# A streaming relu-mean: 127 rows a partition, and the first 128 rows one to a partition

## Chip, cores, metric

One core of one Trainium2 chip. The metric is device time of a run in microseconds (us). All runs were at a granted clock of 1.0. A ratio is the mean time of one kernel's runs over that of the other's of the same rounds, so it is not quite the ratio of the medians that are quoted beside it; brackets give its 95% interval.

## The reference

```python
x = np.random.randn(32, 512, 1024).astype(np.float32)
def reference(x):
    return np.mean(np.maximum(x, 0), axis=-1).astype(np.float32)   # 16384 rows of 1024
```

64 MiB come in, 64 KiB go out, and each element is used once. Loads and stores are moved by 16 DMA engines in packets; a packet here is one contiguous piece, such as the 16 rows of one partition.

## The kernel before

Partition p owns the 128 rows 128p to 128p+127. They are loaded in seven tiles of 16 rows a partition (8.39 MB, one packet of 64 KB a partition) through three buffers, then in pieces of 8, 4, 2, 1 rows and one last row in three column pieces. Odd rows go to VectorE, even rows to ScalarE; each row is one instruction that takes the maximum with zero and sums. GpSimd scales the sums (the last row is scaled in its own instruction). One store of 512 B a partition ends the kernel.

```python
    J = R // P                                   # 128
    xr = xf.rearrange("(p j) d -> p j d", p=P, j=J)
    outr = out.flatten().rearrange("(p j) -> p j", p=P, j=J)
    NB, BUFS = 16, 3
    full = J // NB - 1                           # 7
    row_pieces, col_pieces = [8, 4, 2, 1], [512, 256, 256]
    # ... (cut: buffers and semaphores)
    for t in range(full):
        buf_free(t)                              # waits for ScalarE and VectorE on tile t-3
        load(t, bufs[t % BUFS][:, :, :], xr[:, t * NB:(t + 1) * NB, :])
    # ... (cut: the loads of the pieces)
    nc.gpsimd.memset(scale[:, :], inv).then_inc(pool, 1)

    def rows(i, xt, lo, n, j0):
        nc.scalar.wait_ge(loaded[i], 16)
        nc.vector.wait_ge(loaded[i], 16)
        for k in range(lo, lo + n):
            j = j0 + k
            done = (dve_row if j % 2 else act_row)(nc, xt[:, k, :], sums[:, j:j + 1])
            # ... (cut: the last row of each engine raises its semaphore)
    # ... (cut: finish(), which scales sums into res on GpSimd; the last two rows)
    nc.sync.dma_start(out=outr, in_=res[:, :]).then_inc(stored, 16)
```

The first load is moved ahead of the entry barrier, so it is issued at time 0 of the span.

## Time and profile before

| | before |
|---|---|
| median of 3 runs | 162.33 us (162.28 to 162.63) |
| profiled span | 161.1 us |
| load queue, share of 16 engines' span | 97.3% |
| VectorE / ScalarE busy | 46% / 43% |

The page shows a stream: the load queue is hardly ever idle, and the two compute engines wait for it. The prediction shows the page's lines, the table of stretches and the drain. It lacks the moments at which tiles arrive, by which the kernels are compared later. Here they are for the kernel before, as VectorE's first instruction on each of the first four tiles in the timeline (start, duration, instruction, and in brackets the idle time that the tile's arrival ended):

```profile
22.45 1.22 DVE L20 TENSOR_SCALAR_CACHE_REDUCE rows<-rows 128x1024 f32<-128x1024 f32 x1 [22.45 <-DMA rows<-in_x_dram]
...
41.71 1.22 DVE L20 TENSOR_SCALAR_CACHE_REDUCE rows<-rows 128x1024 f32<-128x1024 f32 x1 [10.05 <-DMA rows<-in_x_dram]
...
61.15 1.22 DVE L20 TENSOR_SCALAR_CACHE_REDUCE rows<-rows 128x1024 f32<-128x1024 f32 x1 [10.24 <-DMA rows<-in_x_dram]
...
81.01 1.22 DVE L20 TENSOR_SCALAR_CACHE_REDUCE rows<-rows 128x1024 f32<-128x1024 f32 x1 [10.65 <-DMA rows<-in_x_dram]
```

From 41.71 to 61.15 is 19.44 us and from 61.15 to 81.01 is 19.86; the later tiles take 19.34 to 19.36. Ten idle microseconds a tile are VectorE's slack.

### The profile page before, as it was taken

What the parts mean: (1) busy time and instruction counts of PE and PEld (TensorE: products, weight loads), DVE (VectorE), ACT (ScalarE), POOL (GpSimd) and SP (SyncE); (2) the same over time, 40 slices, a digit from 0 to 9 for tenths busy, and PEclk for the clock granted to TensorE, in tenths of its full rate; (3) what the DMA queues carried; (4) which work ended last, traced back from release to release, by engine and by line L of the source; (5) the groups of instructions that cost most, each with busy time, mean ns of one, the idle gap of its engine ahead of it and who ended that gap; (6) DMA issues with size and microseconds to landing.
All of it is one profiled execution on the core that took longest, in us unless ns stands there. A gap on an engine that the chain in (4) does not pass through costs nothing. (4 is left out here: it accounts for less than half of the span.)

```text
span 161.1 us, 336 instructions
## 1 busy us (share of the span) xinstructions
DVE 74.3 (46%) x132; ACT 69.2 (43%) x131; POOL 1.3 (1%) x8
## 2 busy tenths in 40 slices
DVE  0000049800696008940089400992029900498994
ACT  3000049600694008920089200990029800496974
POOL 1000000000000000000000000000000000000001
DMA  7997997997997998999999999999999999899991
GB/s 260 521 472 309 521 472 309 521 456 325 521 439 342 521 423 358 525 391 391 521 391 391 505 407 391 505 407 391 505 407 391 505 407 391 382 464 391 409 401 52
DMA packets 2162, 67.19 MB, mean 417 GB/s; under 512 B 240, under 2 KB 624, under 8 KB 880
## 3 DMA queue, kind: packets, MB, share of 16 engines
q1 hardware_dynamic: 2160, 67.18, 97.3%
q14 instruction: 2, 0.02, 0.0%
HBM read 67.11 MB, written 0.07 MB: 417 GB/s over the span
## 5 line engine op out<-in xcount | busy, mean ns | idle before, releaser
L20 DVE TENSOR_SCALAR_CACHE_REDUCE rows<-rows 128x1024 f32<-128x1024 f32 x64 | 73.3, 1208 | 84.8 <-DMA rows<-in_x_dram 84.6
L15 ACT ACTIVATE rows<-rows 128x1024 f32<-128x1024 f32 x64 | 66.2, 1036 | 88.2 <-DMA rows<-in_x_dram 88.0
L15 ACT ACTIVATION_READ_ACCUMULATOR rows<-rows 128x1 f32 x64 | 11.9, 187 | 0.0
L20 DVE DVE_READ_ACCUMULATOR rows<-rows 128x1 f32 x64 | 5.3, 83 | 0.0
L15 ACT ACT_TABLE_LOAD x1 | 1.3, 1283 | 1.4 <-PEq L55 1.4
L132 POOL TENSOR_SCALAR res<-sums 128x112 f32<-128x112 f32 (+1 forms) x2 | 0.5, 250 | 155.5 <-DVE rows L20 155.5
L15 ACT ACTIVATE last<-last 128x512 f32<-128x512 f32 x1 | 0.6, 629 | 0.0
L20 DVE TENSOR_SCALAR_CACHE_REDUCE last<-last 128x256 f32<-128x256 f32 x1 | 0.4, 420 | 0.2 <-DMA last<-in_x_dram 0.2
L165 DVE SCALAR_TENSOR_TENSOR last<-last,scale 128x258 f32<-128x258 f32 x1 | 0.4, 428 | 0.1
L117 POOL MEMSET scale<- 128x258 f32 x1 | 0.3, 313 | 1.0 <-POOLq L55 1.0
L155 POOL TENSOR_SCALAR res<-part 128x1 f32<-128x1 f32 x1 | 0.3, 264 | 0.6 <-DVE rows L20 0.6
L15 ACT ACTIVATION_READ_ACCUMULATOR last<-last 128x1 f32 x1 | 0.2, 186 | 0.0
L195 POOL MEMSET const-bfloat16-1.0<- 128x1 bf16 x1 | 0.1, 102 | 0.0
L195 POOL MEMSET const-uint8-127<- 128x1 uint8 x1 | 0.1, 102 | 0.0
L195 POOL MEMSET const-float32-0.0<- 128x1 f32 x1 | 0.1, 99 | 0.2 <-issue 0.2
L195 POOL MEMSET const-float32-1.0<- 128x1 f32 x1 | 0.1, 99 | 0.0
L20 DVE DVE_READ_ACCUMULATOR last<-last 128x1 f32 x1 | 0.1, 83 | 0.0
L165 DVE DVE_READ_ACCUMULATOR last<-last,scale 128x1 f32 x1 | 0.1, 82 | 0.0
## 6 DMA issues: line engine op xcount, KB each, us to landing
rows<-in_x_dram SPq DMA_DIRECT2D x1, 4096.0 KB, 39.1
rows<-in_x_dram SPq DMA_DIRECT2D x1, 2048.0 KB, 43.6
rows<-in_x_dram SPq DMA_DIRECT2D x1, 1024.0 KB, 45.6
rows<-in_x_dram SPq DMA_DIRECT2D x1, 512.0 KB, 46.5
last<-in_x_dram SPq DMA_DIRECT2D x1, 256.0 KB, 46.6
last<-in_x_dram SPq DMA_DIRECT2D x2, 128.0 KB, 46.4
rows<-in_x_dram SPq DMA_DIRECT2D x7, 49.2
out_dram<-res SPq DMA_DIRECT2D x1, 64.0 KB, 1.5
```

Source lines behind the costliest of these rows:

```text
L15: return nc.scalar.activation(out=src, in_=src, func=ACT.Relu, accum_out=acc)
L20: return nc.vector.tensor_scalar(out=src, in0=src, scalar1=0.0, scalar2=init, op0=ALU.max, op1=ALU.add, accum_out=acc,)
L117: nc.gpsimd.memset(scale[:, :], inv).then_inc(pool, 1)
L132: nc.gpsimd.tensor_scalar(out=res[:, lo:hi], in0=sums[:, lo:hi], scalar1=inv, scalar2=0.0, op0=ALU.mult, op1=ALU.add,)
L155: nc.gpsimd.tensor_scalar(out=res[:, J - 2:J - 1], in0=part[:, 0:1], scalar1=part[:, 1:2], scalar2=inv, op0=ALU.add, op1=ALU.mult,).then_i ...
L165: nc.vector.scalar_tensor_tensor(out=last[:, 768:], in0=last[:, 768:], scalar=0.0, in1=scale[:, :], op0=ALU.max, op1=ALU.mult, accum_out=r ...
L195: nc = _bacc.Bacc("TRN2", target_bir_lowering=False, num_devices=1)
```

## The change

The intent is a row pitch between partitions that is no power of two: 127 rows of 4 KiB (508 KiB) in place of 128 (512 KiB). That leaves 128 rows over. They are loaded one to a partition behind tile 0, averaged by one ScalarE instruction that scales as well, turned from a column into rows by a VectorE transpose, and stored in mid-stream as four runs of 32 results.

```diff
-    xr = xf.rearrange("(p j) d -> p j d", p=P, j=J)
-    outr = out.flatten().rearrange("(p j) -> p j", p=P, j=J)
+    xfirst, xmain = xf[:P, :], xf[P:, :]
+    outfirst, outmain = out.flatten()[:P], out.flatten()[P:]
+    J = J - 1
+    xr = xmain.rearrange("(p j) d -> p j d", p=P, j=J)
+    outr = outmain.rearrange("(p j) -> p j", p=P, j=J)
-    row_pieces = [8, 4, 2, 1]
+    row_pieces = [7, 4, 2, 1]
@@ loads
         load(t, bufs[t % BUFS][:, :, :], xr[:, t * NB:(t + 1) * NB, :])
+        if t == 0:
+            load(-1, row0[:, :], xfirst)
+        if t == BUFS:
+            nc.sync.wait_ge(first, 2)
+            nc.sync.dma_start(
+                out=outfirst.rearrange("(q i) -> q i", i=32), in_=turned0[0:P:32, :],
+            ).then_inc(stored, 16)
@@ compute
+    nc.gpsimd.memset(mean0[:, :], 0.0)
     nc.gpsimd.memset(scale[:, :], inv).then_inc(pool, 1)
+    nc.scalar.wait_ge(pool, 1)
     nc.vector.wait_ge(pool, 1)
     for t in range(full):
         rows(t, bufs[t % BUFS], 0, NB, t * NB)
+        if t == 0:
+            nc.scalar.wait_ge(loaded[-1], 16)
+            nc.scalar.activation(
+                out=row0[:, :], in_=row0[:, :], func=ACT.Relu, scale=inv, accum_out=mean0[:, 0:1],
+            ).then_inc(first, 1)
+            nc.vector.wait_ge(first, 1)
+            nc.vector.transpose(turned0[:, :], mean0[:, :]).then_inc(first, 1)
```

Cut: the three small buffers, one more semaphore and its place in the list that is cleared, the count of full tiles (7 as before), the last row's index, the final wait for 32 in place of 16, an assert.

More of the change, by code (lines that the diff above doesn't have):

```diff
@@ L63 @@
     inv = 1.0 / D
-    xr = xf.rearrange("(p j) d -> p j d", p=P, j=J)
-    outr = out.flatten().rearrange("(p j) -> p j", p=P, j=J)
+    xfirst, xmain = xf[:P, :], xf[P:, :]
[3 more added lines that the diff above has]
+    outr = outmain.rearrange("(p j) -> p j", p=P, j=J)
     NB = 16
     BUFS = 3
-    full = J // NB - 1
-    row_pieces = [8, 4, 2, 1]
-    assert sum(row_pieces) == NB - 1
+    full = J // NB
+    row_pieces = [7, 4, 2, 1]
+    assert full * NB + sum(row_pieces) + 1 == J
     col_pieces = [512, 256, 256]
@@ L84 @@
     scale = sbuf("scale", P, D // 4 + 2)
-    loaded = [nc.alloc_semaphore(f"loaded{i}") for i in range(full + len(row_pieces) + len(col_pieces))]
+    row0, mean0, turned0 = sbuf("row0", P, D), sbuf("mean0", P, 32), sbuf("turned0", P, 32)
+    loaded = [nc.alloc_semaphore(f"loaded{i}") for i in range(full + len(row_pieces) + len(col_pieces) + 1)]
     act, dve, pool = (nc.alloc_semaphore(n) for n in ("act", "dve", "pool"))
+    first = nc.alloc_semaphore("first")
     stored = nc.alloc_semaphore("stored")
@@ L144 @@
     finish(i, j0, j0 + lo)
-    prev = xt[:, NB - 2, :]
+    prev = xt[:, lo, :]
     nc.scalar.wait_ge(loaded[i], 16)
@@ L173 @@
     nc.sync.dma_start(out=outr, in_=res[:, :]).then_inc(stored, 16)
-    used = [s.num for s in (*loaded, act, dve, pool)]
+    used = [s.num for s in (*loaded, act, dve, pool, first)]
     assert used == list(range(used[0], used[0] + len(used)))
     nc.sync.sem_clear(range(used[0], used[-1] + 1))
-    nc.sync.wait_ge(stored, 16).then_inc(stored, -16)
+    nc.sync.wait_ge(stored, 32).then_inc(stored, -32)
     issue_ahead_of_entry_barrier(nc)
```

## The prediction

> **What bounds the kernel now.** I read the page first: busy shares, DMA rows, queue, chain, costly groups, DMA issues.
>
> ```profile
> span 161.1 us, 336 instructions
> DVE 74.3 (46%) x132; ACT 69.2 (43%) x131; POOL 1.3 (1%) x8
> ...
> q1 hardware_dynamic: 2160, 67.18, 97.3%
> ...
> HBM read 67.11 MB, written 0.07 MB: 417 GB/s over the span
> ...
> DVE 0%; issue 0%
> ...
> L20 DVE TENSOR_SCALAR_CACHE_REDUCE rows<-rows 128x1024 f32<-128x1024 f32 x64 | 73.3, 1208 | 84.8 <-DMA rows<-in_x_dram 84.6
> L15 ACT ACTIVATE rows<-rows 128x1024 f32<-128x1024 f32 x64 | 66.2, 1036 | 88.2 <-DMA rows<-in_x_dram 88.0
> ...
> rows<-in_x_dram SPq DMA_DIRECT2D x7, 49.2
> out_dram<-res SPq DMA_DIRECT2D x1, 64.0 KB, 1.5
> ```
>
> Both compute engines are under half busy and nearly all their idle time ends on a load; the load queue is busy for 97.3% of the span. The chain of waits follows the last vector instruction only and says 0%, because it does not follow the loads; it is no help here. So the question is whether the stream itself can go faster. I cut the span at the moments the tiles arrive (first instruction on each tile in the timeline: 22.3, 41.7, 61.1, 81.0, 100.4, 119.7, 139.1 us).
>
> ```profile
> core 0: us, DVE busy (x) ACT busy (x) POOL busy (x), PEclk, DMA share, GB/s
> 22.30:41.70 19.40, 9.21 (x16) 8.42 (x16) 0.00 (x0) 1.00 1.00 432
> 41.70:61.10 19.40, 9.20 (x16) 8.43 (x16) 0.00 (x0) 1.00 1.00 432
> 61.10:81.00 19.90, 9.20 (x16) 8.43 (x16) 0.00 (x0) 1.00 0.98 422
> 81.00:100.40 19.40, 9.23 (x17) 8.46 (x17) 0.00 (x0) 1.00 1.00 432
> ```
>
> A tile of 8.39 MB takes 19.35 to 19.4 us with the DMA engines fully busy; compute on it takes 9.2. One tile takes 19.9. The packet records say why: each of the 16 engines runs 64 KB packets back to back, median 2.418 us, shortest 2.415, so eight packets (8 partitions) make 19.34 us. At 65.06 to 65.46 us two 8 KB instruction fetches were taken in between; one engine lost about 1.0 us there (a gap of 0.4 and a packet of 2.99), and that very engine ends last, at 158.30 us, about 0.3 behind the next. The other loss is at the start: the first packet of each engine, beginning at 1.0 to 2.0 us, takes 2.9 to 3.5 us instead of 2.4. The end is a short drain (timeline):
>
> ```profile
> 158.46 0.42 DVE L20 TENSOR_SCALAR_CACHE_REDUCE last<-last 128x256 f32<-128x256 f32 x1 [0.25 <-DMA last<-in_x_dram]
> ...
> 158.99 0.43 DVE L165 SCALAR_TENSOR_TENSOR last<-last,scale 128x258 f32<-128x258 f32 x1
> ...
> 159.50 0.35 SPq L173 DMA_DIRECT2D out_dram<-res  x1
> ```
>
> Last bytes 158.30, usable 158.99, reduced 159.42, store issued 159.50 and landed 1.5 us later, span end 161.07. The time is about 1.0 us of start, about 157.3 of stream, about 2.8 of drain. Only the stream's bytes and rate, the last piece and the final store can move it.
>
> **What the Trainium skill says.** (1) "DMA: Bandwidth & Descriptors", section "Where 436 GB/s comes from": sixteen ports of 32 B at 850 MHz give 435.2 GB/s, and the ports bind. The trace agrees: 65,536 B in 2.418 us is 27.1 GB/s, times 16 is 433.7, or 99.6% of it. (2) The same page, "Latency and other measured facts": a 512 KiB row pitch gave 207 GB/s in each direction of HBM copies, against 214 when a large pitch was padded by 4 KiB. Here the pitch of the partitions is 128 rows of 4 KiB, exactly 512 KiB, and the change makes it 508 KiB. I take this to be the point of the change. The trace before does not show such a loss: the steady packets run at the port's rate. (3) The same page, "Specifications": below 512 B a transfer is handled with a read-modify-write. The final store writes 128 packets of 512 B, median 27 ns each; no shorter data write exists in this trace to compare. (4) "VectorE: DVE Perf Modes", "The three transpose paths": VectorE transposes independent 32x32 blocks, 311 ns for 128x128 bf16. No transpose is in this trace.
>
> **The change part by part.**
>
> *Pitch.* The main rows start 508 KiB apart. With steady packets at 2.418 us and a port limit of 2.409 (65,536 B over 27.2 GB/s), 64 packet-equivalents an engine can gain at most 64 x 0.009 = 0.6 us, and I expect 0. The slow first packets could be the alias, worth up to 16 engines' common 0.6 us; but the engines stay within about 1 us of each other for the whole stream, as at the start, and later packets are not slow, so I think it is a cold start: -0.1 as an expectation.
>
> *Bytes and packets.* The bytes are the same: 7x16 + 7+4+2+1 + 1 = 127 rows a partition plus one extra row each. The 8-row piece (32 KB packets, 1.213 us) becomes a 7-row piece (28 KB) and a separate 4 KB packet (0.159 us). From 0.159 us at 4 KB and 0.309 at 8 KB a packet has about 9 ns of fixed cost, so 8 more packets an engine are 0.07 us, plus a completion write of 9 ns: +0.08 us, straight on the path.
>
> *First rows.* They arrive behind tile 0 and push tiles 1 to 6 later by 0.52 MB / 433 GB/s = 1.21 us, plus overhead; the 7-row piece then lands where the 8-row piece landed (120 rows ahead of it in both). ScalarE's extra row runs after its eight of tile 0, at 30.7 us, for about 1.04 + 0.19 us; VectorE is done at 31.65, waits until about 32, and transposes in an estimated 0.1 to 0.3 us. Tile 1 is due at 43.0, so 10 us of slack cover it. The buffer is released before these instructions on each engine, so tile 3's issue stays at 31.7. Cost 0.
>
> *Mid-stream store.* SyncE waits for the transpose at about 32.3 and next needs to issue at about 52: no delay. Four packets of 128 B in a queue that is served in order, near 81 us; even a slow one costs one engine perhaps 0.1 us: +0.02 expected.
>
> *Tail compute.* Tile 6 arrives at 140.3 and VectorE needs 9.2, so it ends at 149.5, 0.7 after the 7-row piece lands at 148.8. That piece has four rows on ScalarE and three on VectorE: 148.8 + 4 x 1.04 = 153.0 and 149.5 + 3 x 1.14 = 152.9, before the 4-row piece at 153.7. The lag is gone, and the last 4, 2, 1, 1 rows are as before. Cost 0.
>
> *Final store.* 127 results are 508 B a partition, and rows no longer start on 512 B. If each packet took twice its 27 ns, eight an engine add 0.22 us; if only pipelined, near 0; if a read comes before each write, 0.5. I put +0.2, directly on the end.
>
> Sum: -0.1 + 0.08 + 0.02 + 0.2 = +0.2, or 162.5 us.
>
> **The rivals.** *A. The pitch was costing time.* The skill's copy figures and the slow first packets speak for it; the packet rate against the port limit speaks against it. If the first packets fall to 2.4, -0.6; if the 0.6 of steady margin is won too, -1.2: about 161.2 at best. The 2% line is 159.1, out of reach: all of the start, the fetch and the margin together would not make it.
> *B. The store below 512 B is dear.* If the eight packets of an engine each wait for an HBM read of the skill's 0.2 us, +1.6: 164. The small size and the many engines make it unlikely in full. The 2% line above is 165.6.
> *C. The new pitch is worse,* or engines drift apart more: 1% on the stream would be 163.9. Nothing in the profile speaks for it.
> *D. Fetch luck.* The last engine is last because of the instruction fetch; a few more instructions can move the fetch to another tile or engine: -0.3 to +0.4 without any meaning.
>
> **Range and chances.** The runs of before spread over 0.35 us. Adding D and halves of A and B gives 161.7 to 163.3. Faster by over 2%: 0.02; within: 0.95; slower: 0.03.
>
> **What would show it.** Right: steady tiles at 19.35 to 19.4 us; tile 1 at about 43.0 and the 7-row piece at about 148.8; transpose near 32; last load usable within 0.5 us of 159.0; final store 1.5 to 1.9 us to landing. Wrong: 64 KB packets off 2.418 us either way, first packets at 2.4 (A), a final store over 2 us (B), or a load issued later than its buffer's release because SyncE sat on the new wait.

## The result, and the profile after

The changed kernel took 162.45 us in the median of four runs (162.18 to 162.54) against 162.31 (162.04 to 162.63) of the kernel before: ratio 1.0006 [0.9984, 1.0027], the same within 2% and within noise. Two later sessions gave 0.9993 [0.9980, 1.0005] and 0.9990 [0.9977, 1.0003].

From the page of the changed kernel (span, busy shares, load queue, groups, and DMA issues with size and time to landing; line numbers moved by the inserted code):

```profile
span 160.8 us, 341 instructions
DVE 73.3 (46%) x131; ACT 70.3 (44%) x133; POOL 1.3 (1%) x9
...
q1 hardware_dynamic: 2312, 67.18, 97.4%
...
L20 DVE TENSOR_SCALAR_CACHE_REDUCE rows<-rows 128x1024 f32<-128x1024 f32 (+1 forms) x63 | 72.1, 1208 | 84.0 <-DMA rows<-in_x_dram 83.8
L15 ACT ACTIVATE rows<-rows 128x1024 f32<-128x1024 f32 x64 | 66.2, 1036 | 65.9 <-DMA rows<-in_x_dram 65.7
...
L15 ACT ACT_TABLE_LOAD x1 | 1.3, 1283 | 22.4 <-DMA rows<-in_x_dram 22.4
...
rows<-in_x_dram SPq DMA_DIRECT2D x7, 49.1
```

Queue share, mean durations and the loads' time to landing (49.1 against 49.2) are as before. One line is new and was not predicted: the load of ScalarE's table now waits for tile 0. Before, it ran at 1.44 us; the wait for GpSimd's memset, put ahead of ScalarE's first work, moved it behind the wait for the load, where it costs 1.28 us of ScalarE's slack in tile 0 (e6 undoes this). ScalarE's idle time of 65.9 in place of 88.2 is the same fact: the first 22.4 us are now counted ahead of the table load.

The timeline after tile 0 shows the extra row, the transpose and the store's issue (SPq lines are issues, not transfers):

```profile
31.94 0.19 ACT L15 ACTIVATION_READ_ACCUMULATOR rows<-rows 128x1 f32 x1
32.03 1.04 ACT L158 ACTIVATE row<-row 128x1024 f32<-128x1024 f32 x1
32.15 0.33 SPq L100 DMA_DIRECT2D rows<-in_x_dram  x1
32.98 0.19 ACT L158 ACTIVATION_READ_ACCUMULATOR row<-row 128x1 f32 x1
33.20 0.21 DVE L162 STREAM_TRANSPOSE turned<-mean 128x32 f32<-128x32 f32 x1 [1.53 <-ACT row L158]
33.44 0.63 SPq L116 DMA_DIRECT2D out_dram<-turned  x1
42.95 1.06 ACT L15 ACTIVATE rows<-rows 128x1024 f32<-128x1024 f32 x1 [9.79 <-DMA rows<-in_x_dram]
42.95 1.22 DVE L20 TENSOR_SCALAR_CACHE_REDUCE rows<-rows 128x1024 f32<-128x1024 f32 x1 [9.54 <-DMA rows<-in_x_dram]
```

ScalarE and VectorE are done with it at 33.4 us, the store is issued by 34.1, and the next tile comes at 42.95, as predicted (43.0). The transpose took 0.21 us, within the estimated 0.1 to 0.3. Of the other signs, the tiles after that took 19.36, 19.64, 19.36, 19.36 and 19.34 us, and the 7-row piece landed at 148.5 us (issued at 110.59, 37.9 to landing; predicted 148.8). The drain, from the same timeline:

```profile
158.18 0.42 DVE L20 TENSOR_SCALAR_CACHE_REDUCE last<-last 128x256 f32<-128x256 f32 x1 [0.23 <-DMA last<-in_x_dram]
...
158.71 0.43 DVE L189 SCALAR_TENSOR_TENSOR last<-last,scale 128x258 f32<-128x258 f32 x1
...
159.22 0.35 SPq L197 DMA_DIRECT2D out_dram<-res  x1
```

Each line is about 0.28 us earlier than in the prediction's fence of the kernel before, and from the store's issue to the end of the span it is 1.6 us in both. By the trace's packet records the 508 B packets of the final store took 27 ns in the median, exactly as the 512 B packets did. So the drain is unchanged, and what little moved lies in the stream. The first packets are as slow as before (mean 3.18 us, before 3.12), and the steady median is 2.418 us in both.

The packet records show one difference. (They do not name the engine; where one engine is spoken of, packets were linked end to start.) Leave out each engine's first packet and those around the two mid-stream instruction fetches (8 KB packets of a queue of their own, marked "instruction"), and sum what the 64 KB packets took over 2.418 us. This sum, called the excess below, is 0.36 us an engine before and 0.15 after. Packets of over 2.48 us in that set: 25 before, 9 after. The median cannot show this.

### The profile page after: what moved, and what is told of

The parts are those of the page before. It is cut to its first block, busy times and chain, and to the rows that moved or that the text cites. A ratio compares the mean times of both kernels' runs of the same rounds, so it can differ in the third digit from the quotient of the medians.

```text
span 160.8 us, 341 instructions
## 1 busy us (share of the span) xinstructions
DVE 73.3 (46%) x131; ACT 70.3 (44%) x133; POOL 1.3 (1%) x9
## 5 line engine op out<-in xcount | busy, mean ns | idle before, releaser
L20 DVE TENSOR_SCALAR_CACHE_REDUCE rows<-rows 128x1024 f32<-128x1024 f32 (+1 forms) x63 | 72.1, 1208 | 84.0 <-DMA rows<-in_x_dram 83.8
L15 ACT ACTIVATE rows<-rows 128x1024 f32<-128x1024 f32 x64 | 66.2, 1036 | 65.9 <-DMA rows<-in_x_dram 65.7
L15 ACT ACT_TABLE_LOAD x1 | 1.3, 1283 | 22.4 <-DMA rows<-in_x_dram 22.4
L158 ACT ACTIVATE row<-row 128x1024 f32<-128x1024 f32 x1 | 1.0, 1043 | 0.0
## 6 DMA issues: line engine op xcount, KB each, us to landing
rows<-in_x_dram SPq DMA_DIRECT2D x1, 3584.0 KB, 37.9
rows<-in_x_dram SPq DMA_DIRECT2D x7, 49.1
```

Source lines behind the costliest of these rows:

```text
L15: return nc.scalar.activation(out=src, in_=src, func=ACT.Relu, accum_out=acc)
L20: return nc.vector.tensor_scalar(out=src, in0=src, scalar1=0.0, scalar2=init, op0=ALU.max, op1=ALU.add, accum_out=acc,)
L158: nc.scalar.activation(out=row0[:, :], in_=row0[:, :], func=ACT.Relu, scale=inv, accum_out=mean0[:, 0:1],).then_inc(first, 1)
```

## The experiments

What had to be told apart: is the pitch worth nothing, or does a gain hide the costs? What makes the first packets slow? Are the small costs (packets, short stores, table load, fetch) what I took them for?

**e1: the old pitch under the new instructions.** Its output is wrong, which doesn't matter for the time.

```diff
-    xr = xmain.rearrange("(p j) d -> p j d", p=P, j=J)
+    xr = xf.rearrange("(p j) d -> p j d", p=P, j=J + 1)[:, 1:, :]
```

> The changed kernel with the main rows read at the old pitch of 512 KiB (rows 1 to 127 of each group of 128; the results are wrong on purpose, the instructions are the same). My theory, that the pitch is worth nothing: 64 KB packets 2.418 us in the median, first packets 2.9 to 3.6 us, ratio to the kernel before 1.000 to 1.001 as for the changed kernel. Rival, that the new pitch gains what the added packets and the short store cost: this run keeps the costs without the gain, so it is slower than the changed kernel by 0.3 us or more (ratio 1.002 to 1.004).

162.38 us, ratio 1.0015 [1.0002, 1.0028]. This is between the two expectations. First packets had a mean of 3.09 us, so the first part of the theory held: they do not depend on this pitch. But the excess of the later packets was 0.42 us an engine, with 44 packets over 2.48 us: again more than in the changed kernel. Not decided here.

**e2: partitions 64 KiB apart.** The kernel before with every tile contiguous; results in wrong places on purpose.

```diff
-        load(t, bufs[t % BUFS][:, :, :], xr[:, t * NB:(t + 1) * NB, :])
+        load(t, bufs[t % BUFS][:, :, :], xf[t * NB * P:(t + 1) * NB * P, :].rearrange("(p j) d -> p j d", p=P, j=NB))
```

(and the same for the pieces.)

> The kernel before with every tile read from one contiguous 8 MB, so that the partitions lie 64 KiB apart and not 512 (results in the wrong places on purpose). If the pitch is worth nothing: first packets still 2.9 to 3.6 us, steady packets 2.418, ratio 0.999 to 1.001. If the slow first packets are partitions that collide in HBM: they change with so different a pitch, towards 2.42 us (ratio 0.996), or upwards.

162.12 us, 0.9991 [0.9979, 1.0003]: 0.14 us plus or minus 0.17 faster than the kernel before, from which it differs in addresses alone, so not clear of noise. First packets 3.07 us in the mean: colliding partitions do not make them that slow. Excess 0.13 us an engine. One thing did change at the start: the slowest engine's first packet ended at 4.55 us in place of 5.06, and VectorE began tile 0 at 21.91 us in place of 22.45. This is one profile, of the fastest of the five runs; e12 returns to it.

**e3: the 4 KB rows first.**

```diff
+        if t == 0:
+            load(-1, row0[:, :], xfirst)
         load(t, bufs[t % BUFS][:, :, :], xr[:, t * NB:(t + 1) * NB, :])
-        if t == 0:
-            load(-1, row0[:, :], xfirst)
```

> The changed kernel with the load of the first 128 rows issued ahead of tile 0, so the first packets are 4 KB (0.159 us when steady). If the start costs a fixed latency of about 0.7 us per engine before its queue runs: the 4 KB first packets take 0.7 to 0.9 us and the 64 KB packets after them 2.42; time within 0.2 us of the changed kernel. If the start is slow in proportion, or for as long as some 3 us: first packets 0.2 us, and the 64 KB packets behind them 2.9 us or more. If the pitch of tile 0 makes it: 4 KB packets from contiguous rows at 0.16 us, 64 KB ones slow.

In the trace the eight earliest packets of 4 KB took 1.05 to 1.30 us in place of 0.159, the other engines' first ones started a microsecond later at 0.16 to 0.19, and the 64 KB packets behind them took 2.46 in the mean. So the start is a fixed delay of 0.9 to 1.1 us, not a rate and not the pitch; somewhat more than the 0.7 I had put. The time was a miss: 162.96 us (162.53 to 163.55), ratio 1.0049 [1.0031, 1.0066], against an expected 0.2 us. In the profiled run, the fastest of the six, tile 0 is issued only at 1.44 us and its packets follow the rows' without a gap (SyncE's issues in the timeline; a row of x4 merges four loads):

```profile
0.00 0.38 SPq L100 DMA_DIRECT2D row<-in_x_dram  x1
1.44 32.30 SPq L100 DMA_DIRECT2D rows<-in_x_dram  x4
```

A queue that runs dry after 1.3 us of 4 KB packets, whenever the barrier takes longer, would explain the slower runs; no profile shows one, so it stays open.

**e4: the packet cost, enlarged fifteen times.** The kernel before with tile 1 in 16 loads of a row each (all on one semaphore, waited for at 256; the other tiles and the wait are cut here).

```diff
+        if t == 1:
+            for k in range(NB):
+                load(t, bufs[t][:, k, :], xr[:, t * NB + k, :])
```

> The kernel before with tile 1 loaded by 16 loads of one row a partition, so 128 packets of 4 KB an engine in place of 8 of 64 KB. By my term of 9 ns a packet plus 9 ns a completion write: 120 x 9 + 15 x 9 = 1.2 us more, ratio 1.0075. If the extra packets are hidden (packets overlap): ratio 1.000 to 1.002. If each packet has a gap beside its 9 ns: 2 us or more, ratio 1.012 or more.

163.39 us, 1.0073 [1.0061, 1.0085]: 0.0073 x 162.2 = 1.18 us, where the term of 9 ns a packet and a completion write gave 1.2. The page shows the loads (the 16, and the one-row piece that has the same size) and the packet count, 2162 before:

```profile
DMA packets 4322, 67.19 MB, mean 415 GB/s; under 512 B 480, under 2 KB 864, under 8 KB 3168
...
rows<-in_x_dram SPq DMA_DIRECT2D x17, 512.0 KB, 23.0
```

So by this term the change's eight extra packets an engine and one completion write (the 4 B packet that ends each load on an engine) cost 0.08 us, and they do lie on the path. The interval leaves 1.0 to 1.4 us for e4.

**e5: the changed kernel again.**

> The changed kernel itself once more, as the yardstick beside the other three kernels of this call and for a second profile. If its added packets (0.08 us) are all that the change costs: ratio to the kernel before 1.0005, within 1.000 to 1.0015. If the 508 KiB pitch gives back a little: packets of 64 KB over 2.48 us stay at about a dozen as in its first profile (27 in the kernel before, 46 in e1), and the ratio is 1.000 or just below.

162.17 us against 162.29, 0.9993 [0.9980, 1.0005]; 3 packets over 2.48 us outside the fetches, excess 0.10 us an engine. The second expectation fits; the first's value of 1.0005 is the upper end of the interval, so this run alone does not exclude it.

**e6: the table load back at the start.**

```diff
-    nc.scalar.wait_ge(pool, 1)          # ahead of tile 0
+            nc.scalar.wait_ge(pool, 1)  # ahead of the first rows' activation
```

> The changed kernel with ScalarE's wait for the memset moved from ahead of tile 0 to just ahead of the first rows' activation, so the table load (1.28 us) goes back to about 1.4 us from 22.4. Theory, that ScalarE has slack: the extra row's activation starts at 30.7 and not 32.0, tile 3 is issued 0.4 us earlier, and the time stays within 0.1% of the changed kernel of the same call. Rival, that the late table load cost something the change gained elsewhere: faster than the changed kernel by 0.3 us or more.

From its timeline: the table load, and SyncE's issues of the mid-stream store and of the loads around it.

```profile
1.45 1.28 ACT L15 ACT_TABLE_LOAD   x1 [1.45 <-PEq L55]
...
31.90 0.63 SPq L116 DMA_DIRECT2D out_dram<-turned  x1
52.04 60.16 SPq L100 DMA_DIRECT2D rows<-in_x_dram  x7
```

The store is issued 1.5 us earlier than in the changed kernel, the next loads 0.2 us earlier, and the time is 162.13 us, ratio 0.9993, to the fourth digit that of the changed kernel in the same session. The two means differ by 0.01 us, plus or minus 0.13: no cost of the late table load shows.

**e7: a small last store.** The kernel before, which stores seven tiles' means when they are ready and only the last 16 columns at the end.

```diff
     nc.sync.wait_ge(pool, 2)
+    nc.sync.dma_start(out=outr[:, :j0], in_=res[:, :j0]).then_inc(stored, 16)
+    nc.sync.wait_ge(pool, 3)
     nc.sync.wait_ge(dve, n_done + 2)
-    nc.sync.dma_start(out=outr, in_=res[:, :]).then_inc(stored, 16)
+    nc.sync.dma_start(out=outr[:, j0:], in_=res[:, j0:]).then_inc(stored, 16)
     # ... (cut: the first seven tiles' scaling raises pool; the final wait is for 32)
```

> The kernel before with the means of the first seven tiles (448 B a partition) stored when ready, and only the last 16 columns (64 B a partition) in the final store. If short stores cost nothing extra: last packets about 11 ns each, the final store's packets over in 0.2 us and not 0.35, ratio 0.999 to 1.000. If a store below 512 B is dear where it is far below: final store over 2 us, ratio 1.003 or more.

162.06 us, 0.9986 [0.9973, 0.9998]. The DMA issues of its page, with landing times (before: one of 64.0 KB, 1.5 us):

```profile
out_dram<-res SPq DMA_DIRECT2D x1, 56.0 KB, 10.2
out_dram<-res SPq DMA_DIRECT2D x1, 8.0 KB, 1.4
```

Packets of 448 B took 25 ns and of 64 B 11 ns, and the final packets were over in 0.21 us against 0.35. No penalty below 512 B shows at any size tried; of the store's 1.4 us to landing the packets are 0.21. The gain is 0.21 us plus or minus 0.16 here and 0.11 plus or minus 0.18 in e11.

**e8: fewer instructions, to be rid of the fetch.** In tiles 0 to 5 of the kernel before, ScalarE takes five rows, VectorE four as before and seven by two wide instructions.

```diff
+        nc.vector.tensor_scalar(out=xt_[:, 9:, :], in0=xt_[:, 9:, :], scalar1=0.0, scalar2=None, op0=ALU.max).then_inc(wide, 1)
+        # ... four single rows between, and a wait on wide
+        nc.vector.tensor_reduce(out=sums[:, j_ + 9:j_ + 16], in_=xt_[:, 9:, :], op=ALU.add, axis=mybir.AxisListType.X).then_inc(dve, 1)
```

> The kernel before with fewer instructions on ScalarE and VectorE: in tiles 0 to 5 ScalarE takes five rows, VectorE four as before and seven by one maximum and one sum over all seven. Theory, that the last DMA engine is last because it carried an instruction fetch of 8 KB in mid-stream: with one or both fetches gone the slowest engine ends nearer the others, and the ratio is 0.997 to 0.9985 with both gone. Rival, that the spread between engines is there anyway (they start up to 1 us apart): ratio 0.999 to 1.001, whether or not the fetches go. VectorE's busy time a tile should rise from 9.2 us to 13 to 18, still under the 19.4 of a tile; if it passes that, the time grows.

Its page, and its table for tile 0's stretch (from, to, length, busy of VectorE, ScalarE and GpSimd with counts, clock, DMA share, GB/s):

```profile
span 160.8 us, 264 instructions
DVE 115.0 (72%) x96; ACT 50.5 (31%) x95; POOL 1.3 (1%) x8
```

```profile
22.30:41.70 19.40, 15.98 (x10) 5.30 (x10) 0.00 (x0) 1.00 1.00 432
```

The work fits under the stream even with VectorE at 16.0 us a tile, but both 8 KB fetches are still there, only later (84.2 and 89.1 us in place of 65.1 and 65.2). So the theory was not tested: 162.20 us, 0.9994 [0.9980, 1.0008]. In this profile one of the fetches fell on the engine that had been the fifth from the front, and it still ended last, 0.23 us behind the next. What the fetch costs in time stays open.

**e9 and e10: the pitch, in one session.** The changed kernel and e1's kernel again, six runs of each.

> The changed kernel in one call with its twin at the old pitch (next run). In ten profiles so far the 64 KB packets outside the two fetches took 0.26 to 0.42 us an engine over their steady 2.418 us in the five kernels with 512 KiB pitch, and 0.08 to 0.15 in the five with 508 or 64. If that 0.2 to 0.25 us reaches the end of the kernel, this run is faster than its twin by about 0.2 us (0.1 to 0.3), and its ratio to the kernel before is about 0.999. Rival, that it is lost in the spread between engines or is an accident of the profiles: twin and this within 0.05 us.

> The changed kernel's instructions at the old pitch of 512 KiB, wrong results on purpose, in the same call. Pitch matters: about 162.4 us, ratio 1.0005 to 1.0015, over 0.26 us an engine of excess in its 64 KB packets. Pitch doesn't matter: ratio as the changed kernel's within 0.0003.

e9: 162.17 us, 0.9990 [0.9977, 1.0003]. e10: 162.44 us, 1.0007 [0.9991, 1.0022]. Twin against twin, the means differ by 0.30 us, plus or minus 0.19 (1.96 standard errors of six runs each), at the upper end of the 0.1 to 0.3 expected. The arrivals of tiles 1 to 3 on VectorE, first e9 (508 KiB):

```profile
42.99 1.22 DVE L20 TENSOR_SCALAR_CACHE_REDUCE rows<-rows 128x1024 f32<-128x1024 f32 x1 [9.55 <-DMA rows<-in_x_dram]
62.35 1.22 DVE L20 TENSOR_SCALAR_CACHE_REDUCE rows<-rows 128x1024 f32<-128x1024 f32 x1 [10.15 <-DMA rows<-in_x_dram]
81.92 1.22 DVE L20 TENSOR_SCALAR_CACHE_REDUCE rows<-rows 128x1024 f32<-128x1024 f32 x1 [10.36 <-DMA rows<-in_x_dram]
```

then e10 (512 KiB):

```profile
43.12 1.22 DVE L20 TENSOR_SCALAR_CACHE_REDUCE rows<-rows 128x1024 f32<-128x1024 f32 x1 [9.67 <-DMA rows<-in_x_dram]
62.58 1.22 DVE L20 TENSOR_SCALAR_CACHE_REDUCE rows<-rows 128x1024 f32<-128x1024 f32 x1 [10.25 <-DMA rows<-in_x_dram]
82.35 1.22 DVE L20 TENSOR_SCALAR_CACHE_REDUCE rows<-rows 128x1024 f32<-128x1024 f32 x1 [10.57 <-DMA rows<-in_x_dram]
```

Tile 0 came at 22.49 and 22.51 us. The twin at the old pitch is 0.13 us late at tile 1, 0.23 at tile 2 and 0.43 at tile 3, and from there on both take about 19.36 us a tile: VectorE's column piece of the last row comes 0.44 us later. The interval from tile 2 to 3 holds the fetches and is noisier than the others. Over all profiles, with each run's own fetches left out (which moves a few of the figures quoted in e9's expectation), the excess of the 64 KB packets was 0.23 to 0.42 us an engine in the seven profiles at 512 KiB (e4 with one tile less) and 0.08 to 0.22 in the seven at 508 or 64 KiB. The two groups all but touch (e8 0.227, e12 0.222), and the count of packets over 2.48 us does not part them: e4 had 3 and e8 had 6 at 512 KiB, against 9 in the first profile of the changed kernel. What parts them better is when the excess falls: before 60 us it was 0.12 to 0.37 us an engine at 512 KiB and 0.00 to 0.10 at the others, after 60 us 0.05 to 0.12 in both.

**e11 and e12: a version that is right and faster.** e12 is e7's kernel with contiguous tiles (no row left over, so no extra load) and an output order to match; e11 is e7 again as its twin.

```diff
+    xtail = xf[j0 * P:, :].rearrange("(p j) d -> p j d", p=P, j=NB)     # the last 16 rows a partition
+        load(t, bufs[t % BUFS][:, :, :], xf[t * NB * P:(t + 1) * NB * P, :].rearrange("(p j) d -> p j d", p=P, j=NB))
+    nc.sync.dma_start(out=out.flatten()[:j0 * P].rearrange("(t p j) -> p t j", p=P, j=NB),
+        in_=res[:, :j0].rearrange("p (t j) -> p t j", j=NB)).then_inc(stored, 16)
+    nc.sync.dma_start(out=out.flatten()[j0 * P:].rearrange("(p j) -> p j", p=P, j=NB), in_=res[:, j0:]).then_inc(stored, 16)
     # ... (cut: the lines that these replace, the loads of the pieces from xtail, and e7's waits)
```

> The kernel before with the early store and the 64 B final store, at 512 KiB pitch, as the twin of the next run: ratio 0.9985 as in e7 (0.0015 is 0.24 us, of which the final packets explain about 0.15).

> A version meant to be right and faster than both: every tile is one contiguous 8 MB (partitions 64 KiB apart, no extra row load), the first seven tiles' means are stored early as 64 B runs, the last 16 columns in a 64 B final store. If the pitch matters in the time: faster than its twin e11 by about 0.2 us, ratio to the kernel before about 0.997. If not: as e11. If the 896 packets of 64 B of the early store get in the way of the last loads: slower than e11.

e11: 162.25 us, 0.9992 [0.9978, 1.0005]. e12: 161.97 us, 0.9978 [0.9966, 0.9990], correct, 0.22 us plus or minus 0.14 faster than e11 and 0.2 us below the changed kernel of the same session in the mean. Its early store is out of the way although it moves 896 packets of 64 B:

```profile
out_dram<-res SPq DMA_DIRECT2D x1, 56.0 KB, 10.6
out_dram<-res SPq DMA_DIRECT2D x1, 8.0 KB, 1.4
```

So the layout of the loads showed in two pairs of twins, one of which has neither the extra rows nor the transpose: 0.30 and 0.22 us, about 0.15% of the time. The second pair also differs in the packets of the early store. Nor do its arrivals repeat those of e9 and e10. First e11 (tiles 0, 2 and 3):

```profile
22.55 1.22 DVE L20 TENSOR_SCALAR_CACHE_REDUCE rows<-rows 128x1024 f32<-128x1024 f32 x1 [22.55 <-DMA rows<-in_x_dram]
...
61.14 1.22 DVE L20 TENSOR_SCALAR_CACHE_REDUCE rows<-rows 128x1024 f32<-128x1024 f32 x1 [10.15 <-DMA rows<-in_x_dram]
...
80.93 1.22 DVE L20 TENSOR_SCALAR_CACHE_REDUCE rows<-rows 128x1024 f32<-128x1024 f32 x1 [10.58 <-DMA rows<-in_x_dram]
```

then e12:

```profile
21.98 1.22 DVE L20 TENSOR_SCALAR_CACHE_REDUCE rows<-rows 128x1024 f32<-128x1024 f32 x1 [21.98 <-DMA rows<-in_x_dram]
...
60.56 1.22 DVE L20 TENSOR_SCALAR_CACHE_REDUCE rows<-rows 128x1024 f32<-128x1024 f32 x1 [10.14 <-DMA rows<-in_x_dram]
...
80.69 1.22 DVE L20 TENSOR_SCALAR_CACHE_REDUCE rows<-rows 128x1024 f32<-128x1024 f32 x1 [10.91 <-DMA rows<-in_x_dram]
```

With contiguous tiles the whole lead is there at tile 0 (0.57 us, as in e2), stays until tile 2 (0.58) and shrinks over the fetches to 0.24 at tile 3 (0.28 at the last row's column piece). In both profiles at 64 KiB the slowest engine's first packet ended at 4.55 to 4.60 us, and tile 0 came at 21.9 to 22.0; in the others that start with tile 0 these were 4.79 to 5.17 and 22.2 to 22.6. So the start is the same for 508 and 512 KiB in the twins e9 and e10, but not for 64; why is not shown. And 64 KiB is a power of two as well, so it is not that property alone that made 512 KiB slower.

## Why the prediction was right, and which terms were not

The call was right: the stream runs at its port's rate, as the prediction works out from the skill's figure, nothing in the change touches that, and the time stayed within 2% and inside the range. Its terms, one by one:

- **Pitch, taken as 0 in the steady stream and -0.1 at the start.** Wrong in size and in place. The twins at the changed kernel's pitch give -0.30 us (the contiguous tiles of e12 -0.22, in another place). At 508 KiB little of it can be at the start: first packets took 2.8 to 3.3 us in the mean of a run at every pitch, e3 shows a fixed delay, and tile 0 came at 22.46 us against 22.45 before, and at 22.49 against 22.51 in the twins. (In e5 and e6 it came at 22.16 and 22.23, so the -0.1 there is not excluded.) The loss at 512 KiB is in scattered packets of the first half of the stream, most of them before 60 us. The step that failed is "later packets are not slow", with the margin "64 x 0.009": it took the median packet as if it were the mean, and the records of the kernel before already held 25 slow ones and an excess of 0.36 us. Why the 512 KiB pitch makes them, and why they stop, no run shows.
- **Packets, +0.08.** Right; e4 measured the same term fifteen times over.
- **First rows and transpose, 0.** Right, though 1.2 us late (transpose at 33.2, predicted near 32), because I overlooked that the new wait drags the table load along. e6 shows that this, too, is slack. Tile 3 was issued at 32.1 and not at 31.7 us, which is as harmless.
- **Mid-stream store, +0.02.** Its four packets took 13 ns each, at 80.4 to 81.5 us. Right.
- **Tail compute, 0.** Right: the lag behind tile 6 is gone by 152.6 us on VectorE and 152.8 on ScalarE (predicted 152.9 and 153.0), and the 4-row piece comes at 153.42.
- **Final store, +0.2.** Wrong: 0. The 508 B packets took 27 ns as the 512 B ones. So rival B did not show either; the 0.2 us in it is the average HBM access latency of "DMA: Bandwidth & Descriptors", "Latency and other measured facts", and its +1.6 an estimate from that.

Three smaller readings of the prediction do not come out of the records, and none of them moves the call. The engine with the worst fetch lost 0.87 us (a gap of 0.30 and 0.57 in the next packet), not about 1.0. The first packets were 0.70 us over the steady ones in the mean, not 0.6. And 162.5 with D and halves of A and B gives about 161.6 to 163.7, not 161.7 to 163.3; the result lies in both.

Measured terms in the sum: -0.30 (e9 against e10) + 0.08 + 0 = -0.22 us, give or take 0.2, where the prediction had +0.2. The three sessions gave +0.1, -0.1 and -0.2 us (1.0006, 0.9993 and 0.9990 of 162.3), and -0.22 lies within the interval of each. The forecast stood because its two errors, 0.2 us too little for the pitch and 0.2 too much for the store, are small beside a range of 1.6; they add up, and the centre of 162.5 was about 0.4 us too high by the terms, 0.05 to 0.3 by the medians. The fetch (rival D) was seen in every profile, on one or two engines each; whether it moves the time was not settled.

## What to carry to other kernels

In this stream, whose DMA engines were fully busy (share 1.00 in steady tiles), changes of layout were worth tenths of a percent. To see so little, compare a twin that differs in the addresses alone, in the same session, and look at the sum of the packets' excess and at the arrivals of all tiles, the first included, not at the packets' median. Count what a rearrangement adds beside its gain; here contiguous tiles gained without left-over rows. And a wait placed ahead of an engine's first work can move its table load behind that engine's first data, so check where such set-up went.

## What the Trainium skill lacked or had wrong

- "DMA: Bandwidth & Descriptors", "Specifications", read-modify-write below 512 B: no cost of it showed. Packets took 27 ns at 512 and 508 B, 25 at 448, 13 at 128, 11 at 64, and the final store landed in 1.5 us at 512 B and 1.4 at 64 B. The page gives no such figures for small stores on this chip.
- The same page, "Latency and other measured facts", row pitch: its figures are for copies in both directions (207 GB/s at 512 KiB against 214 at a padded pitch, 3%). For reads alone the 512 KiB pitch cost 0.30 us of 162 against 508 KiB and 0.22 against contiguous tiles, under 0.2%; the page has no number for a one-way load.
- The same page gives about 600 ns as first-byte latency of this path ("Latency and other measured facts"). The first packets were longer by 0.4 to 0.9 us (64 KB, means of a run) and by 0.9 to 1.1 us (4 KB, eight engines); whether this is the same quantity the runs do not show.
- "Runtime: NRT & Kernel Launch", "Instruction fetch mechanics", calls the cost of such a fetch "mostly hidden", but does not tell what it does to loads in flight: around two of 8 KB, two DMA engines lost 0.63 and 0.87 us in the trace of the kernel before.
- "ScalarE: Activation LUTs", "What ACT_TABLE_LOAD costs", has its duration right (1283 ns, measured 1283), but not that a semaphore wait ahead of the first activation can put it behind the wait for the data (22.41 in place of 1.44 us).
